# A hybrid SSD / DeltaNet layer on one core: the first two projection blocks read x itself, and u is formed in place while the second one runs

## The chip, the cores and the metric

The kernel runs on one core of a Trainium2 chip. The metric is the device time of one execution in microseconds (us). Five instruction streams run side by side and wait for each other through semaphores: TensorE (PE), VectorE (DVE), ScalarE (ACT), GpSimd (POOL) and SyncE (SP), which issues most of the DMAs.

## The reference, cut to what matters

Only the start of the layer is touched: the RMS norm of the input, and the first columns of the one input projection. 336 tokens (16 meta, 256 prompt, 64 sample) of 2048 channels go in.

```python
def _rmsnorm(x, w):
    xf = xf * lax.rsqrt(jnp.mean(xf * xf, axis=-1, keepdims=True) + EPS)
    return (xf * w.astype(jnp.float32)).astype(x.dtype)
...
    u = _rmsnorm(x, norm_mix_w)
    z_a, xbc_a, dt_a, qkv_b, z_b, beta_b, a_b, gate_a, gate_b = jnp.split(u @ w_in, SPLIT_IDX, axis=-1)
    xbc, conv_a_new = _causal_conv(xbc_a, conv_a, ssd_conv_w, ssd_conv_b)
    xbc = jax.nn.silu(xbc).astype(f32)
```

With r the root of a token and w the norm weight, u = x * r * w. So u @ W equals r times (x @ (w * W)): the weight can go into W, and the root, which is one number for each token, can be applied to the product.

## The kernel before

Everything that PE multiplies in the big projections is split in two: a float32 value v becomes hi (v rounded to fp32r by ACT) and lo (v - hi by DVE), and a product is three matmuls, hi*hi, hi*lo and lo*hi. The stream of weights is cut in chunks `n` of 512 rows by 256 columns. `wload(n)` issues the DMA of a chunk into a tile `raw` on SP, and `wsplit(n)` makes `hi` (one ACT instruction) and `lo` (one DVE instruction) of it. There are three buffers each of `raw`, `hi` and `lo`, so chunk n is loaded when the `lo` of chunk n-3 has been formed. `block()` multiplies four chunks (16 k of 128 channels) by the transposed activations `uh`, `ul` (channels on partitions, 336 tokens) into two PSUM tiles `pbig`: 24 matmuls for a chunk, 96 for a block. The first block of all takes the k in order with both column tiles in turn; later ones take the four k of a chunk for one column tile and then for the other.

`proj_ssd(0)`, the generator `main0`, runs five such blocks: two for the x part of the first SSD group (they end in a convolution, `conv_a`), one for B and C, two for z. The first block is interleaved by hand with the preparation (under `manual_schedule`, so all engines keep the written order there); from the second block on `run(main0, side)` puts steps of `side` between the matmuls, by the numbers that `side` yields, PE keeps the written order, and a scheduler decides the order on the other engines.

The preparation: x is loaded in three pieces of 112 tokens, transposed on PE (`flip`) and copied into `xT`; the sums of squares (`sumsq`) go through `root` (a power on POOL) and `spread_d` (a diagonal matrix `dgx` on DVE) to PE, which spreads the roots over all partitions (`prx`, copied to `rbx`). Then, for each k, `u_scale` multiplies `xT` by `rbx` (on DVE for even k, on POOL for odd k) and `u_split` forms `uh` (ACT) and `ul` (DVE). Only then can the matmuls of that k start. Behind the first block come the transposes of the convolution weights and states (`load_cols` of `cra`, `crb`, `sra`, `srb`), the 32 matmuls `ptok` for the small dt/beta/a columns, and then the second block. `tokens()` turns `ptok` into decays (`pcum`, `prow`), writes them to DRAM (`rowd`, DMA on ACT) and the scan of the first group reads them back (`eab`, `em`), with the SSD state `sio` behind them on SP (PE turns it: `psi`). `scratch()` writes `xT` to DRAM (`xTd`) for the residual.

## Time and profile before

| | us |
|---|---|
| median of 3 runs | 2344.87 (2339.98 to 2345.06) |
| the profiled execution | 2343.37 |
| its span | 2341.5 |
| PE busy in the span | 2300.9 (98%) |
| DVE / ACT / POOL busy | 1354.5 / 1065.4 / 333.1 |
| first matmul of the first block starts | 21.36 |
| last matmul of the first block starts | 46.54 |

PE is busy for nearly the whole span; it is not in the first 48 us. A profile row gives start, duration, engine, source line, operation, output and input tiles, and in brackets how long the engine sat idle before it and what ended that. A duration can hold time in which the instruction was stalled after its start.

### The profile page before, as it was taken

The page shows a single profiled execution, that of the slowest core. Times are in us where ns is not written, and L with a number is a line of the kernel's source. Part 1 is how long each engine was busy: PE and PEld are TensorE (multiplying, and loading weights), DVE is VectorE, ACT ScalarE, POOL GpSimd, SP SyncE. Part 2 cuts the span into 40 slices and gives each one's busy share as a digit, 9 for nine tenths or more (in the row PEclk, how much of TensorE's full clock was granted, in tenths as well). Part 3 has the DMA queues.
Part 4 walks back from the last instruction along what each step waited for, and adds up shares of the span by engine and source line. Part 5 has one row for each costly group of instructions (what it writes and reads, how often), then busy time and mean ns, then how long its engine had stood idle before and what let it go on. Part 6 is the DMA issues. An engine that isn't in the chain of part 4 may idle for free.

```text
span 2341.5 us, 40643 instructions
## 1 busy us (share of the span) xinstructions
PE 2300.9 (98%) x16393; PEld 2278.7 (97%) x16393; DVE 1354.5 (58%) x2147; ACT 1065.4 (46%) x1830; POOL 333.1 (14%) x488
## 2 busy tenths in 40 slices
PE   7999999999999999999999999999999999999997
PEld 6999999999999999999999999999999999999997
DVE  6675757575765547668668567444444444444444
ACT  5664545455445545554554445433343244234433
POOL 3142414141121112112212110000000000000000
PEclk9999999999999999999999999999999999999999
DMA  7845454546565555645556644544544454445543
GB/s 193 224 131 161 136 174 126 173 124 179 157 199 172 151 163 137 163 147 144 144 149 161 171 142 145 151 150 151 148 152 153 146 152 153 146 152 151 166 143 117
DMA packets 411046, 362.87 MB, mean 155 GB/s; under 512 B 48329, under 2 KB 407834, under 8 KB 410394
## 3 DMA queue, kind: packets, MB, share of 16 engines
q1 hardware_dynamic: 410746, 360.15, 52.8%
q8 instruction: 128, 2.10, 0.4%
...
q10 hardware_dynamic: 112, 0.13, 0.0%
...
## 4 chain that ended last, share of the span: by engine, by line
PE 90%; DVE 5%; DMA 2%; ACT 1%; issue 1%; SPq 1%; POOL 0%; ACTq 0%; DVEq 0%
PE pbig L58 84%; DVE lo L64 1%; DMA raw<-in_w_in_dram 1%; PE po L58 1%; DVE pr L64 1%; DVE ubt L858 1%; PE pS L58 0%; DVE c L67 0%; PE pyd L58 0%; PE pw L58 0%; PE pkk L58 0%; PE pqk L58 0%; ACT hi L61 0%; PE ph L58 0%; DMA x<-in_x_sample_dram 0%
## 5 line engine op out<-in xcount | busy, mean ns | idle before, releaser
L64 DVE TENSOR_TENSOR lo<-raw,hi 128x1024 fp32r<-128x1024 f32 x591 | 738.2, 1250 | 711.2 <-ACT hi L61 705.1
L61 ACT ACTIVATE hi<-raw 128x1024 fp32r<-128x1024 f32 x592 | 627.5, 1060 | 890.4 <-PE pbig L58 840.1
L58 PE MATMUL pbig<-uh,hi 128*128 128x320 f32 (+2 forms) x2176 | 689.2, 317 | 4.2 <-ACT uh L61 4.2
L58 PE MATMUL pbig<-ul,hi 128*128 128x320 f32 (+2 forms) x2176 | 682.5, 314 | 4.0 <-DVE ul L67 3.9
L58 PE MATMUL pbig<-uh,lo 128*128 128x320 f32 (+2 forms) x2176 | 681.0, 313 | 0.7 <-DVE lo L64 0.7
L58 PEld LDWEIGHTS pbig<-uh,hi 128*128 128x128 f32 x2176 | 411.3, 189 | 10.0 <-ACT uh L61 4.7
L58 PEld LDWEIGHTS pbig<-ul,hi 128*128 128x128 f32 x2176 | 411.5, 189 | 6.0 <-DVE ul L67 5.8
L58 PEld LDWEIGHTS pbig<-uh,lo 128*128 128x128 f32 x2176 | 411.4, 189 | 1.0 <-DVE lo L64 1.0
L58 PE MATMUL pbig<-hh,hi 128*128 128x320 f32 x1024 | 318.0, 311 | 0.0
L58 PE MATMUL pbig<-hnl,hi 128*128 128x320 f32 x1024 | 317.1, 310 | 0.0
L58 PE MATMUL pbig<-hl,hi 128*128 128x320 f32 x1024 | 316.2, 309 | 0.0
L58 PE MATMUL pbig<-hh,lo 128*128 128x320 f32 x1024 | 316.2, 309 | 0.0
L58 PE MATMUL pbig<-hnh,lo 128*128 128x320 f32 x1024 | 315.8, 308 | 0.0
L58 PE MATMUL pbig<-hnh,hi 128*128 128x320 f32 x1024 | 315.1, 308 | 0.0
L58 PEld LDWEIGHTS pbig<-hnh,lo 128*128 128x128 f32 x1024 | 192.9, 188 | 0.0
L58 PEld LDWEIGHTS pbig<-hl,hi 128*128 128x128 f32 x1024 | 192.6, 188 | 0.0
L58 PEld LDWEIGHTS pbig<-hh,hi 128*128 128x128 f32 x1024 | 192.6, 188 | 0.0
L58 PEld LDWEIGHTS pbig<-hnh,hi 128*128 128x128 f32 x1024 | 192.3, 188 | 0.2
L58 PEld LDWEIGHTS pbig<-hh,lo 128*128 128x128 f32 x1024 | 192.5, 188 | 0.0
L58 PEld LDWEIGHTS pbig<-hnl,hi 128*128 128x128 f32 x1024 | 192.2, 188 | 0.0
L58 PE MATMUL pbig<-yh,hi 128*128 128x320 f32 x512 | 161.2, 315 | 1.1 <-ACT yh L61 1.1
L58 PE MATMUL pbig<-yl,hi 128*128 128x320 f32 x512 | 157.6, 308 | 0.3 <-DVE yl L64 0.3
...
## 6 DMA issues: line engine op xcount, KB each, us to landing
raw<-in_w_in_dram SPq DMA_DIRECT2D x256, 512.0 KB, 3.9
raw<-in_w_up_dram SPq DMA_DIRECT2D x128, 512.0 KB, 3.9
raw<-in_w_down_dram SPq DMA_DIRECT2D x128, 512.0 KB, 3.5
...
raw<-in_w_in_dram SPq DMA_DIRECT2D x32, 256.0 KB, 3.5
...
```

The source lines that it names most:

```text
L58: nc.tensor.matmul(out, lhsT=lhsT, rhs=rhs, start=start, stop=stop, **kw)
L61: nc.scalar.activation(out=out, in_=in_, func=func, **kw)
L64: eng.tensor_tensor(out=out, in0=a, in1=b, op=op)
L858: V.tensor_reduce(out=ubt[:NE, j0:, s], in_=v, axis=AX.X, op=ADD)
```

## The change: what it does

- The first two blocks (chunks 0 to 7, `NRAW = 8`) multiply x, not u. `flip` now forms `uh` and `ul` straight from the transposes in PSUM (ACT, then DVE). `wsplit` of these eight chunks puts the norm weight into hi and lo: four ACT and four DVE instructions of 256 columns, one for each k, where there was one of 1024 each.
- The root is applied at the end of the two blocks: `conv` gets `rb=rbx` and multiplies the PSUM tiles by `rbx` on DVE, where ACT copied them.
- x comes in pieces of 128, 128 and 80 tokens, the last one in two halves of its columns. Chunk 0 is loaded ahead of the last piece. The small rows (`prow`, and the convolution weights and states) are loaded first, by DMAs on ACT, and are turned between the transposes of x. `warmer` puts 6, 3 and 3 matmuls of the identity on PE.
- `whole_x` makes `xT` (x itself) again as uh + ul on POOL, four instructions of 1344 columns. The sums of squares, `root` and `spread` now lie between the matmuls of the first block.
- `renorm`, a side generator ahead of `tokens()`, forms u in `uh` and `ul` while the second block runs: for each k a product by `rbx` (POOL, every fourth on DVE), `uh` on ACT, `ul` on DVE, each over the k that the second block has used up. `ptok` moves into `tokens()`, behind `renorm`.

```diff
         lo = wpool.tile([P, 4, 256], F32R, tag="lo", name="lo", bufs=3)
-        tt(G if n == 3 else V, lo, raws[n], hi.bitcast(F32), SUB)
+        if n < NRAW:
+            for k in range(4):
+                w = par[:, NM + n % 4 * 4 + k:NM + n % 4 * 4 + k + 1]
+                act(hi[:, k, :], raws[n][:, k, :], AF.Copy, scale=w)
+                stt(lo[:, k, :], raws[n][:, k, :], w, hi[:, k, :].bitcast(F32), MUL, SUB)
+        else:
+            act(hi, raws[n])
+            tt(V, lo, raws[n], hi.bitcast(F32), SUB)
         split[n] = hi, lo
+    NRAW = 2 * KD // 4
...
-    segs = [[(0, "meta", 0, 16), (16, "pr", 0, 96)], [(0, "pr", 96, 112)], [(0, "pr", 208, 48), (48, "sa", 0, 64)]]
+    X_LO, XS = (0, P, 2 * P), (P, P, NT - 2 * P)
+    segs = [[(0, "meta", 0, 16), (16, "pr", 0, 112)], [(0, "pr", 112, 128)], [(0, "pr", 240, 16), (16, "sa", 0, 64)]]
     src = {"meta": i["meta_tokens"], "pr": i["x_prompt"][0], "sa": i["x_sample"][0]}
-    def load_x(n):
+    xs = [xp.tile([P, D], F32, name=f"x{n}") for n in range(3)]
+    HD = D // 2
+    def load_x(n, c0=0, c1=D):
         for p0, s, r0, nr in segs[n]:
-            nc.sync.dma_start(xs[n][p0:p0 + nr, :], src[s][r0:r0 + nr, :])
-    for n in range(3):
-        xs.append(xp.tile([112, D], F32, name=f"x{n}"))
+            nc.sync.dma_start(xs[n][p0:p0 + nr, c0:c1], src[s][r0:r0 + nr, c0:c1])
...
+    prow = sp0.tile([73, P], F32, name="prow")
+    for r0, name, nr in ((NM, "norm_mix_w", 16), (SN, "ssd_norm_w", 16), (NP_, "norm_mlp_w", 16), (CB_, "ssd_conv_b", 24), (GN, "gdn_norm_w", 1)):
+        nc.scalar.dma_start(prow[r0:r0 + nr, :], i[name][0].rearrange("(t c) -> t c", c=P))
+    turned = []
+    for dst, source, n in ((cwa, i["ssd_conv_w"][0], 96), (sta, i["state_ssd_conv"][0, 0], 72), (cwb, i["gdn_conv_w"][0], 96), (stb, i["state_gdn_conv"][0, 0], 72)):
+        flat = source.rearrange("k (t c) -> (k t) c", c=P)
+        cols = dst.rearrange("p k t -> p (k t)")
+        for r0 in range(0, flat.shape[0], n):
+            row = sp0.tile([96, P], F32, name=f"row{len(turned)}")
+            nc.scalar.dma_start(row[:n, :], flat[r0:r0 + n, :])
+            turned.append((cols[:, r0:r0 + n], row, n))
     load_x(0)
     load_x(1)
-    prow = sp0.tile([73, P], F32, name="prow")
-    for r0, name, nr in ((NM, "norm_mix_w", 16), (SN, "ssd_norm_w", 16), (NP_, "norm_mlp_w", 16), (CB_, "ssd_conv_b", 24), (GN, "gdn_norm_w", 1)):
-        nc.sync.dma_start(prow[r0:r0 + nr, :], i[name][0].rearrange("(t c) -> t c", c=P))
-    load_x(2)
-    warm = sp0.tile([P, 1], F32, name="warm")
-    act(warm, ones[:, 0:1], AF.Square)
+    wload(0)
+    load_x(2, 0, HD)
+    load_x(2, HD, D)
+    wload(1)
+    wload(2)
...
+    def warmer(n):
+        ps = scr("pwarm")
+        for _ in range(n):
+            mm(ps[:, :P], ident, ident)
...
+    def flip(n, k):
+        x0, w = X_LO[n], XS[n]
+        ps = scr("pu").rearrange("p (k t) -> p k t", k=4)[:, :, :w]
+        for m in range(4):
+            transp(ps[:, m, :], xs[n][:w, (k + m) * P:(k + m + 1) * P])
+        h, l = uh[:, k:k + 4, x0:x0 + w], ul[:, k:k + 4, x0:x0 + w]
+        act(h, ps)
+        tt(V, l, ps, h.bitcast(F32), SUB)
...
+        r = rsx[:XS[n], n:n + 1]
+        V.tensor_scalar(out=r, in0=ssx[:XS[n], n:n + 1], scalar1=1.0 / D, scalar2=EPS, op0=MUL, op1=ADD)
+        tt(G, r, r, nhalf_pow[:XS[n], 0:1], ALU.pow)
+        V.tensor_scalar(out=dgx[:XS[n], n, :XS[n]], in0=ident[:XS[n], :XS[n]], scalar1=r, scalar2=None, op0=MUL)
+    def spread():
+        prx = scr("prx")
+        for n in range(3):
+            mm(prx[:, X_LO[n]:X_LO[n] + XS[n]], ones[:XS[n], :], dgx[:XS[n], n, :XS[n]])
+        act(rbx, prx[:, :NT])
+    un = [flat[:, k * NT:(k + 1) * NT] for k in range(KD - 1)] + [sp0.tile([P, NT], F32, name="un")]
...
+    def whole_x(q):
+        tt(G, xT[q], uh[:, q * 4:q * 4 + 4, :].bitcast(F32), ul[:, q * 4:q * 4 + 4, :].bitcast(F32), ADD)
+    def renorm():
+        yield 4.9
+        for k in range(KD):
+            w = par[:, NM + k:NM + k + 1]
+            tt(V if k % 4 == 3 else G, un[k], xT[k // 4][:, k % 4, :], rbx, MUL)
+            act(uh[:, k, :], un[k], AF.Copy, scale=w)
+            stt(ul[:, k, :], un[k], w, uh[:, k, :].bitcast(F32), MUL, SUB)
+            yield 1.0
...
+        if rb is None:
+            act(t[:, 3 + n0:275], ps[:, 0:272 - n0])
+            act(t[:, 278:342], ps[:, 272 - n0:336 - n0])
+        else:
+            tt(V, t[:, 3:275], ps[:, 0:272], rb[:, 0:272], MUL)
+            tt(V, t[:, 278:342], ps[:, 272:336], rb[:, 272:336], MUL)
...
-                conv_a(pt[j], g * 4 + b * 2 + j, x4[:, b * 2 + j, :])
+                conv_a(pt[j], g * 4 + b * 2 + j, x4[:, b * 2 + j, :], 0, None if g else rbx)
...
-    for k in range(4):
-        u_scale(k)
+    warmer(6)
+    load_cols(par, prow, 73)
+    for t in turned[:2]:
+        load_cols(*t)
+    for k in range(0, KD, 4):
+        flip(0, k)
+    for t in turned[2:]:
+        load_cols(*t)
+    warmer(3)
+    for k in range(0, KD, 4):
+        flip(1, k)
+    wsplit(0)
+    warmer(3)
+    flip(2, 0)
+    flip(2, 4)
     for k in range(KD):
-        u_split(k)
-        if k + 4 < KD:
-            u_scale(k + 4)
-        if k % 4 == 1 and k < KD - 4:
-            wsplit(k // 4 + 1)
         for _ in range(2 if k < KD - 1 else 1):
             next(main0)
+        if k == 0:
+            wsplit(1)
+        elif k == 1:
+            flip(2, 8)
+        elif k == 2:
+            flip(2, 12)
+            sumsq(act, 0)
+        elif k == 3:
+            sumsq(V, 1)
+            for q in range(4):
+                whole_x(q)
+            root(0)
+        elif k == 4:
+            wsplit(2)
+            sumsq(act, 2)
+        elif k == 7:
+            root(1)
+            wsplit(3)
+        elif k == 9:
+            root(2)
+        elif k == 12:
+            spread()
+            wsplit(4)
     manual.close()
     hold[0] = len(stream)
...
+        yield 8.0
+        ptok = scr("ptok")
+        for n in range(2):
+            w, wr = wt[:, n * 8:(n + 1) * 8, :], sp.tile([P, 8, P], F32R, tag="wtr", name="wtr", bufs=2)
+            act(wr[:, :, 0:64], w)
+            tt(V, wr[:, :, 64:], w, wr[:, :, 0:64].bitcast(F32), SUB)
+            for k in range(8):
+                mm(ptok[:, :NT], wr[:, k, :], uh[:, n * 8 + k, :], n == 0 and k == 0, False)
+                mm(ptok[:, :NT], wr[:, k, :], ul[:, n * 8 + k, :], False, n == 1 and k == 7)
+        tokT = sp.tile([P, NT], F32, name="tokT")
+        act(tokT, ptok[:, :NT])
+        yield 2.0
...
-    run(main0, chain(tokens(), scratch()))
+    run(main0, chain(renorm(), tokens(), scratch()))
```

**Where the roots are formed.** DVE in the changed kernel, in the first block, from the last split of x to the `lo` of chunk 2 (`lo_381`); `dgx` is the diagonal of the first piece's roots:

```order
L64 TENSOR_TENSOR ul_88<-pu_350,uh_87 128x4x80 [waits Activation_49]
L364 SCALAR_TENSOR_TENSOR acc_89,ssx_187<-x1_146 128x2048 [waits DMAHW4_49]
L368 TENSOR_SCALAR rsx_188<-ssx_187 128x1 [waits Activation_49]
L370 TENSOR_SCALAR dgx_189<-ident_74,rsx_188 128x128 [waits Pool_49]
L67 SCALAR_TENSOR_TENSOR lo_381<-raw_181,par_90,hi_380 128x256 [waits DMAHW4_49,Activation_49]
```

POOL at the same place; the two last kinds of row are the powers of the roots for which `dgx` waits:

```order
L64 TENSOR_TENSOR xT_183<-uh_87,ul_88 128x1344 [waits DVE_49]
L64 TENSOR_TENSOR xT_184<-uh_87,ul_88 128x1344 [waits DVE_49]
L64 TENSOR_TENSOR xT_185<-uh_87,ul_88 128x1344 [waits DVE_49]
L64 TENSOR_TENSOR xT3_186<-uh_87,ul_88 128x1344 [waits DVE_49]
L64 TENSOR_TENSOR rsx_188<-rsx_188,nhalf_pow_83 128x1 [waits DVE_49] x2
L64 TENSOR_TENSOR rsx_188<-rsx_188,nhalf_pow_83 80x1 [waits DVE_49]
```

Before, the roots stood ahead of the first block on both engines, with no 1344-column instruction on POOL and no `lo` of a running block behind a `dgx`. Now `lo_381` stands behind the first `dgx`, which stands behind a power that stands behind all four `whole_x`.

**The start of the second block.** DVE in the changed kernel, from the first row that uses `rbx`: `acc` is the scaled x of k = 3 and 7, `lo_465` is chunk 4, `pre` takes the finished first block, `lo_536` is chunk 5, `c` is the convolution:

```order
L64 TENSOR_TENSOR acc_89<-xT_183,rbx_190 128x336 [waits Activation_49]
L67 SCALAR_TENSOR_TENSOR lo_465<-raw_372,par_90,hi_464 128x256 [waits DMAHW1_49,PE_49,Activation_49]
L64 TENSOR_TENSOR acc_89<-xT_184,rbx_190 128x336
L67 SCALAR_TENSOR_TENSOR lo_465<-raw_372,par_90,hi_464 128x256 [waits Activation_49] x3
L64 TENSOR_TENSOR pre0_116<-pbig_311,rbx_190 128x272 [waits PE_49]
L64 TENSOR_TENSOR pre0_116<-pbig_311,rbx_190 128x64
L64 TENSOR_TENSOR pre1_117<-pbig_312,rbx_190 128x272 [waits PE_49]
L64 TENSOR_TENSOR pre1_117<-pbig_312,rbx_190 128x64
```

And directly behind these:

```order
L67 SCALAR_TENSOR_TENSOR lo_536<-raw_422,par_90,hi_535 128x256 [waits DMAHW3_49,Activation_49]
L67 SCALAR_TENSOR_TENSOR c_512<-pre0_116,cwa_91,c_512 128x339 [waits Activation_49]
L67 SCALAR_TENSOR_TENSOR lo_536<-raw_422,par_90,hi_535 128x256
L67 SCALAR_TENSOR_TENSOR c_512<-pre0_116,cwa_91,c_512 128x339 [waits DVE_49]
L67 SCALAR_TENSOR_TENSOR c_524<-pre1_117,cwa_91,c_524 128x339 [waits Activation_49]
L67 SCALAR_TENSOR_TENSOR c_512<-pre0_116,cwa_91,c_512 128x339 [waits DVE_49]
L67 SCALAR_TENSOR_TENSOR c_524<-pre1_117,cwa_91,c_524 128x339 [waits DVE_49]
L67 SCALAR_TENSOR_TENSOR lo_536<-raw_422,par_90,hi_535 128x256
L67 SCALAR_TENSOR_TENSOR c_524<-pre1_117,cwa_91,c_524 128x339 [waits DVE_49]
L67 SCALAR_TENSOR_TENSOR lo_536<-raw_422,par_90,hi_535 128x256
```

Before, these `lo` were one instruction each and the convolution of the first block came between whole ones. Now the quarters of chunk 5 lie between single steps of the convolution, with five of these ahead of the third quarter; POOL runs its twelve products by `rbx` in the same stretch.

**The loads of x.** SP before, from its start:

```order
L293 DMA x0_145<-in_meta_tokens_dram 16x2048
L293 DMA x0_145<-in_x_prompt_dram 96x2048
L293 DMA x1_146<-in_x_prompt_dram 112x2048
L301 DMA prow_151<-in_norm_mix_w_dram 16x128
L301 DMA prow_151<-in_ssd_norm_w_dram 16x128
```

SP in the changed kernel, from its start:

```order
L304 DMA x0_145<-in_meta_tokens_dram 16x2048
L304 DMA x0_145<-in_x_prompt_dram 112x2048
L304 DMA x1_146<-in_x_prompt_dram 128x2048 [waits DMAHW4_49]
L198 DMA raw_173<-in_w_in_dram 128x4x256 [waits DMAHW6_49]
L304 DMA x2_147<-in_x_prompt_dram 16x1024 [waits DMAHW7_49]
L304 DMA x2_147<-in_x_sample_dram 64x1024 [waits DMAHW0_49]
```

The second piece of x now waits for a DMA semaphore, `DMAHW4`, on which PE also waits ahead of the transposes of the first piece; everything else on SP stands behind it.

## Rows read from the trace of the kernel before

**Rows 1.** The page, part 1: busy us, share, instructions.
```profile
PE 2300.9 (98%) x16393; PEld 2278.7 (97%) x16393; DVE 1354.5 (58%) x2147; ACT 1065.4 (46%) x1830; POOL 333.1 (14%) x488
```

**Rows 2.** Windows of the span: busy us (instructions) by engine, PEclk, DMA share, GB/s.
```profile
20.00:30.00 10.00, 7.85 (x37) 7.07 (x38) 9.86 (x13) 7.81 (x15) 6.81 (x6) 0.83 0.30 80
40.00:50.00 10.00, 7.43 (x37) 6.98 (x38) 5.07 (x15) 5.10 (x11) 0.95 (x4) 0.83 1.12 273
...
110.00:120.00 10.00, 10.00 (x73) 9.98 (x71) 3.28 (x3) 5.63 (x7) 0.00 (x0) 1.00 0.59 169
```

**Rows 3.** Waits of PE, 0 to 150 us: total us, times, longest.
```profile
PE pbig L58 <- ACT uh L61: 4.2, 2, 2.3
PE pbig L58 <- DVE ul L67: 3.9, 4, 2.1
...
PE pcum L58 <- DVE la L64: 0.5, 1, 0.5
```

**Rows 4.** Timeline of PE: the first block, its spacing, its end, and what follows.
```profile
21.36 0.42 PE L58 MATMUL pbig<-uh,hi 128*128 128x336 f32 x1 [2.30 <-ACT uh L61]
...
28.05 0.32 PE L58 MATMUL pbig<-uh,lo 128*128 128x336 f32 x1
28.20 0.32 PE L58 MATMUL pbig<-ul,hi 128*128 128x336 f32 x1
...
46.54 0.32 PE L58 MATMUL pbig<-ul,hi 128*128 128x336 f32 x1
...
48.40 0.40 PE L58 MATMUL ptok<-uh,wtr 128*128 128x336 f32 x1
```

**Rows 5.** Timeline of PE: the first transposes of two pieces of x.
```profile
6.91 1.73 PE L87 MATMUL pu<-ident,x 112*128 112x112 f32 x16 [1.64 <-DMA x<-in_x_prompt_dram]
10.12 1.72 PE L87 MATMUL pu<-ident,x 112*128 112x112 f32 x16 [1.48 <-DMA x<-in_x_prompt_dram]
```

**Rows 6.** Timeline of SP: the issue of the prompt's rows of both pieces.
```profile
1.26 0.87 SPq L293 DMA_DIRECT2D x<-in_x_prompt_dram  x2
```

**Rows 7.** Timeline of DVE and ACT: durations of instructions that the change uses.
```profile
7.53 1.16 DVE L351 COPY xT<-pu 128x448 f32<-128x448 f32 x2 [7.53 <-PE pu L87]
...
10.00 2.29 DVE L326 SCALAR_TENSOR_TENSOR acc<-x 112x2048 f32<-112x2048 f32 x1 [0.94 <-DMA x<-in_x_prompt_dram]
...
10.72 1.85 ACT L61 ACTIVATE xT<-pu 128x448 f32<-128x448 f32 x4 [0.85 <-PE pu L87]
...
17.32 0.28 DVE L340 TENSOR_SCALAR dgx<-ident,rsx 112x112 f32<-112x112 f32 x1 [0.29 <-POOL rsx L64]
...
17.54 1.22 DVE L64 TENSOR_TENSOR lo<-raw,hi 128x1024 fp32r<-128x1024 f32 x1
...
31.79 1.04 DVE L67 SCALAR_TENSOR_TENSOR ul<-ut,par,uh 128x336 fp32r<-128x336 f32 x2
```

**Rows 8.** Timeline of DVE, from 32.7 us.
```profile
32.75 1.23 DVE L64 TENSOR_TENSOR ut<-xT,rbx 128x336 f32<-128x336 f32 x1
33.91 3.13 DVE L67 SCALAR_TENSOR_TENSOR ul<-ut,par,uh 128x336 fp32r<-128x336 f32 x2
```

**Rows 9.** Timeline of POOL: a power, three products, and a whole `lo`.
```profile
16.73 0.55 POOL L64 TENSOR_TENSOR rsx<-rsx,nhalf_pow 112x1 f32<-112x1 f32 x1 [3.61 <-DVE rsx L336]
19.62 3.47 POOL L64 TENSOR_TENSOR ut<-xT,rbx 128x336 f32<-128x336 f32 x3 [2.33 <-ACT rbx L61]
...
32.43 1.19 POOL L64 TENSOR_TENSOR ut<-xT,rbx 128x336 f32<-128x336 f32 x1 [1.34 <-DVE ul L67]
33.58 2.61 POOL L64 TENSOR_TENSOR lo<-raw,hi 128x1024 fp32r<-128x1024 f32 x1
```

**Rows 10.** Timeline: the decay rows' write on ACT, their first read on SP.
```profile
80.67 0.35 ACTq L586 DMA_DIRECT2D rowd<-rows  x1
...
83.46 0.58 SPq L612 DMA_DIRECT2D eab<-rowd  x1
```

**Rows 11.** DMA issues by line: count, KB, us to landing.
```profile
sio<-in_state_ssd_dram SPq DMA_DIRECT2D x4, 256.0 KB, 6.0
```

More of the change, by code (lines that the diff above doesn't have):

```diff
@@ L318, in tile_hybrid_step @@
+    ssx = sp0.tile([P, 3], F32, name="ssx")
+    rsx = sp0.tile([P, 3], F32, name="rsx")
+    dgx = sp0.tile([P, 3, P], F32, name="dgx")
     rbx = sp0.tile([P, NT], F32, name="rbx")
-    HD = D // 2
-    def sumsq(f, x, d0, n):
-        d = junk[:, d0:d0 + x.shape[1]]
+    def flip(n, k):
[6 more added lines that the diff above has]
+        tt(V, l, ps, h.bitcast(F32), SUB)
@@ L323, in sumsq @@
+    def sumsq(f, n):
+        x, d, s = xs[n][:XS[n], :], flat[:XS[n], n % 2 * D:(n % 2 + 1) * D], ssx[:XS[n], n:n + 1]
         if f is act:
-            act(d, x, AF.Square, accum_out=ssx[:, n:n + 1])
+            act(d, x, AF.Square, accum_out=s)
         else:
-            V.scalar_tensor_tensor(out=d, in0=x, scalar=1.0, in1=x, op0=MUL, op1=MUL, accum_out=ssx[:, n:n + 1])
-    def flip(n, k):
-        ps = scr("pu").rearrange("p (k t) -> p k t", k=4)[:, :, :112]
-        for m in range(4):
-            transp(ps[:, m, :], xs[n][:, (k + m) * P:(k + m + 1) * P])
-        return xT[k // 4][:, :, n * 112:(n + 1) * 112], ps
@@ L334, in root @@
-    def root(n):
-        r = rsx[:, n:n + 1]
-        V.tensor_scalar(out=r, in0=ssx[:, n:n + 1], scalar1=1.0 / D, scalar2=EPS, op0=MUL, op1=ADD)
-        tt(G, r, r, nhalf_pow[:112, 0:1], ALU.pow)
-    def spread_d(n):
-        V.tensor_scalar(out=dgx[:, n, :], in0=ident[:112, :112], scalar1=rsx[:, n:n + 1], scalar2=None, op0=MUL)
-    manual = ExitStack()
-    manual.enter_context(tc.manual_schedule())
-    pw_ = scr("pwarm")
-    for n in range(8):
-        mm(pw_[:, :P], ident, ident)
-    prx = psb.tile([P, 512], F32, tag="big", name="prx")
@@ L349, in tile_hybrid_step @@
-    sumsq(act, xs[0], 0, 0)
-    for k in range(0, KD, 4):
-        (V.tensor_copy if k < 8 else act)(*flip(0, k))
-    root(0)
-    sumsq(V, xs[1], D, 1)
-    for k in range(0, KD, 4):
-        act(*flip(1, k))
-    root(1)
-    load_cols(par, prow, 73)
-    for n in range(3):
-        wload(n)
-    sumsq(act, xs[2][:, :HD], 0, 2)
-    sumsq(V, xs[2][:, HD:], D, 3)
-    tt(V, ssx[:, 2:3], ssx[:, 2:3], ssx[:, 3:4], ADD)
-    root(2)
-    spread_d(0)
-    spread_d(1)
-    act(*flip(2, 0))
-    late = [flip(2, k) for k in (4, 8, 12)]
@@ L368, in tile_hybrid_step @@
-    spread_d(2)
-    wsplit(0)
-    for n in range(3):
-        mm(prx[:, n * 112:(n + 1) * 112], ones[:112, :], dgx[:, n, :])
-    act(rbx, prx[:, :NT])
-    for a in late:
-        act(*a)
-    xctx.close()
-    sp = start.enter_context(tc.tile_pool(name="sp", bufs=1))
-    ut = {}
-    def u_scale(k):
-        ut[k] = sp0.tile([P, NT], F32, tag="ut", name="ut", bufs=6)
-        tt(G if k % 2 else V, ut[k], xT[k // 4][:, k % 4, :], rbx, MUL)
-    def u_split(k):
-        t, w = ut.pop(k), par[:, NM + k:NM + k + 1]
-        act(uh[:, k, :], t, AF.Copy, scale=w)
-        stt(ul[:, k, :], t, w, uh[:, k, :].bitcast(F32), MUL, SUB)
+            V.scalar_tensor_tensor(out=d, in0=x, scalar=1.0, in1=x, op0=MUL, op1=MUL, accum_out=s)
@@ L504, in tile_hybrid_step @@
     nc.sync.dma_start(wt[:, :, 32:64], win[:, C_BETA:C_BETA + 32].rearrange("(k p) c -> p k c", p=P))
-    ptok = psb.tile([P, 512], F32, tag="big", name="ptok")
-    for n in range(2):
-        w, wr = wt[:, n * 8:(n + 1) * 8, :], wpool.tile([P, 8, P], F32R, tag="hi", name="wtr", bufs=3)
-        act(wr[:, :, 0:64], w)
-        tt(V, wr[:, :, 64:], w, wr[:, :, 0:64].bitcast(F32), SUB)
-        for k in range(8):
-            mm(ptok[:, :NT], wr[:, k, :], uh[:, n * 8 + k, :], n == 0 and k == 0, False)
-            mm(ptok[:, :NT], wr[:, k, :], ul[:, n * 8 + k, :], False, n == 1 and k == 7)
-    tokT = sp.tile([P, NT], F32, name="tokT")
-    act(tokT, ptok[:, :NT])
-    def tokens():
-        yield 1.0
+    def tokens():
+        yield 8.0
[10 more added lines that the diff above has]
+        yield 2.0
         for c in range(3):
```

38 lines of the change are left out of this document (10 added, 28 removed).

## The prediction

> **What bounds the kernel now.** I read the busy table first: PE is busy for 98% of the span [rows 1], so over most of the 2341.5 us only less work on PE could help, and the change takes none away. What it can win is PE's idle time at the start. There, the timeline of PE shows the first block's first matmul at 21.36 us and its last one at 46.54 [rows 4]. The block is 96 matmuls that follow each other every 0.155 us at full clock [rows 4], so 14.9 us of work lasted 25.5. The list of PE's waits says for what: for `uh` on ACT (4.2 us, of which 2.3 stand ahead of the first matmul) and for `ul` on DVE (3.9) [rows 3]. The windows show the rest: in 20 to 30 and in 40 to 50 us the granted clock is 0.83, so part of each stretch ran at the lower level (1.2 GHz, not 2.4), which costs 0.17 x 10 = 1.7 us each time [rows 2], both times behind a pause of PE. Behind the block the conv transposes end only when `ptok` starts at 48.40 [rows 4]. From there on PE has work without a gap, but for 0.5 us ahead of `pcum` [rows 3]; a window at 110 us shows it full [rows 2].
>
> So I compare one point: the end of the second block, without `ptok` (which moves). Before it stands at 48.40 + 14.9, and with the later 0.5 us at **63.8 us**. Whatever the changed kernel reaches there earlier or later, it keeps to the end.
>
> **The start of the first block.** Before, x had to be whole and normed. Now the block waits for transposes and splits alone. The second piece of x decides. Before, both pieces were issued at 1.26 us [rows 6], and PE could turn them at 6.9 and 10.1 [rows 5]. Now the second piece's DMA waits for the first one's landing (the order on SP), at about 6.8 us, and then needs what the first needed, 6.91 - 1.26 = 5.65, for 1024 KB where that had 896: between 5.65 (the same) and 6.5 us (by size) more, I take 5.8. It lands at 12.6, 2.5 us later than before. Then DVE is the chain: four splits from PSUM of 512 columns at 0.66 each (a copy of 448 took 0.58; ACT's half of one is 0.46 [rows 7], and hidden), with 1.0 for PE and ACT ahead of the first; four quarters of `lo` at 0.40 (a 1024-column `lo` took 1.22 and a 336-column step 0.52, so 256 columns come to 0.45 in the row, 0.40 from start to start); two splits of 80 tokens at 0.45. 12.6 + 1.0 + 2.6 + 1.6 + 0.9 = 18.7 us. PE's first matmul comes at about 17.3, its third, which needs the last split, at 18.3. The first two chunks (2 x 3.7), two more transposes (0.6) and a low-clock stretch (1.7) take it to **27.7 us**. Up to here the change wins some 4 us.
>
> **Chunk 2 waits for the roots.** Its `lo_381` stands on DVE behind `dgx`, that behind a power on POOL, and that behind four `whole_x`. POOL and DVE take turns where both read two tiles in SBUF: at 32.75 a product on DVE of half a microsecond lasted 1.23 because POOL's was running, POOL's whole `lo` then seems to last 2.61, of which it waited 0.4 for that product, and DVE's next two steps last 3.13 in place of 1.04 [rows 8, 9, 7]. So POOL's 1024 columns cost 2.2, and three products of 336 that took turns with DVE's lasted 3.47 [rows 9], which leaves 0.7 for one once DVE's turns of 0.45 are taken off. From 336 to 1024 that is 2.1 ns a column: a `whole_x` of 1344 is an estimated 2.8 us. From 18.7 us on, one after the other because each blocks or waits for the next: `whole_x` 2.8, a quarter of chunk 1's `lo` 0.4, `whole_x` 2.8, three quarters 1.2, the split of x that the third `whole_x` needs 0.45, `whole_x` 2.8, DVE's sum of squares 2.3 [rows 7], `whole_x` 2.8, the power 0.55 [rows 9], `dgx` 0.3 [rows 7], the first quarter 0.4. Sum 16.8: `lo_381` is there at **35.5**, and PE has waited 7.8 us.
>
> Perfetto Trace Analysis, section GPSIMD Engine Instruction, of the Trainium skill says that a GpSimd span in a profile isn't to be trusted and that start-to-start spacing is. Taking the spans as they stand (2.61 for 1024 columns, so 3.4 for a `whole_x`) the four would cost 2.6 us more; [rows 8, 9] speak for the shorter price.
>
> Then come chunks 2 and 3 (7.4) and `prx` (0.65): block one ends at 43.5. `rbx` is ready 2.2 us earlier, at 41.3, because three k are still to be multiplied. The other two roots come in time: chunk 3's `lo` is formed by 39.
>
> **The second block.** From 41.3 on POOL runs its twelve products (0.7 each), and in DVE's order every step with two SBUF inputs takes a turn with them. DVE needs six such turns (the products for k = 3 and 7, the quarters of `lo_465`), some 6.1 to 6.8 us in all, before the fourth quarter is there; PE wants it after 3.9: 2.5 us of waiting. Then four products from PSUM (1.25, no turn), and the third quarter of `lo_536` stands behind two quarters and five steps of the convolution, with POOL's last five products in between: 14.6 us after `rbx`, the fourth at 15.6. PE, late as it already is, wants the fourth at 10.1: 5.3 us of waiting. From chunk 6 on DVE is ahead again. So the block takes 14.9 + 2.5 + 5.3 = 22.7, and ends at 66.2. The 8 extra quarter splits, the root on `pre` and the removed ACT copies cost nothing else: DVE has until the third block for them. In the third block `ul` of k = 11 is late by some 0.9 us.
>
> **Low clock.** PE now pauses for 7.8 us and later for 4.0 in one piece. Before, each low stretch cost 1.7 us and stood behind a pause of about 2 us, though not every such pause had one. I count one whole and one at half: 2.6, which takes up the 0.9 of the third block. Bounds 0.9 and 3.4.
>
> **The scan.** `ptok` and `tokens()` now come one and a half blocks later. `prow` then stands only 51 matmuls (7.5 us, at 0.148) ahead of `psi`. For `psi` the rows must be copied and written, then read: before, the first read was issued 2.8 us after the write [rows 10]; with 1.5 for the copies, two reads are issued at 4.3 after `prow`, and `sio` behind them at 5.5. `sio` lands between 2.8 (the time from the write to that read, the nearest short DMA) and 6.0 us later [rows 10, 11], at 8.3 to 11.5, and PE wants it at 8.0. I take 1.0 us, with bounds of 0 and 3.5.
>
> **Sum.** 66.2 + 2.6 + 1.0 - 63.8 = **+6.0 us** on the profiled execution's 2343.4 us: **2349.4 us**. That execution lies 1.5 us under the median of the runs shown, so I take its own time. A change under 0.3% (7 us) can't be told from none in a measurement of this kernel; the forecast is a slight loss inside that.
>
> **Rivals.**
> *Faster: POOL and DVE don't block each other.* Then `whole_x` 1 and 2 run beside the quarters, the third starts at 24.4, the last ends at 30.0, and with the power, `dgx` and a quarter `lo_381` comes at 31.2: PE waits 3.5, and in the second block 0.4. The point is reached at 31.2 + 8.05 + 15.3 = 54.6, with the clock's 1.7 to 56.3: -7.5, with the scan's 1.0 -6.5 to -8, some **2336 us**. It would take that the long rows on DVE had another cause. Against it: both directions are in [rows 8, 9], and the sums close. SBUF, section Who interferes with whom, of the Trainium skill states the lock as exclusive for a DVE instruction with two SBUF inputs against a GpSimd one that reads; the trace agrees, 3.13 for 1.04. For it: the overlap of the two engines is seen in few rows, none with an instruction as long as `whole_x`. Chance 0.17.
>
> *Slower: the state is late for `psi`.* Place: `prow`, `rowd`, `eab`, `sio`. If the reads take the 6.0 us that the page gives for `sio` [rows 11], PE waits 3.5 instead of 1.0, and a pause of that length can bring another low stretch (1.7): +4.2, **2353.6 us**. It decides from a landing later than 8.0 us after `prow`. Before, `prow` was two blocks and a half ahead, and nothing waited. Chance 0.23.
>
> *The change doesn't do what it says*, that is, PE's first matmul is no earlier: if the second piece lands 3 us later than I take, the chain shifts as a whole, +3: 2352. Chance 0.1; the loss is then the forecast's with another first term.
>
> *Forecast*, 0.5.
>
> **How the numbers follow.** The forecast has a spread of about 5 us (landing 1.5, clock 1.7, POOL's price 2, turns 2): some four tenths of its 0.5 lie above +7 us, which is 0.21, and six tenths of the second and third rivals' 0.33, which is 0.19: slower by over 0.3%, 0.40. Faster by over 0.3%: the first rival's 0.17 and 0.01 of the rest, 0.18. Within 0.3%: 0.42. The range, 2335 to 2357, reaches to the first rival's time and to the second's with its spread; 0.1 is left out at either end.
>
> **What would show it.** The second piece's transposes at 12 to 13.5 us; the first matmul at 16.5 to 18.5; a single wait of PE of 6 to 9 us in the middle of the first block, put down to DVE `lo`, with POOL's four 1344-column rows in front of it; a second group of waits for `lo`, 6 to 9 us in all, in the second block; `psi` waiting for a DMA. The forecast is wrong if POOL's rows lie beside DVE's full-speed rows (first rival), if the wait for `lo_381` is under 4 us, or if the first matmul comes before 15 us: each would bring the time under 2343. If the stalls are there and the time is still lower, I have missed an idle stretch of the kernel before.

## The result, and the profile after

The changed kernel takes **2362.93 us** (median of 4 runs, 2359.57 to 2366.08) against 2342.43 us of the kernel before on the same chip (2339.41 to 2345.06): ratio 1.0088, 95% interval 1.0063 to 1.0113. It is 20.5 us slower. The forecast, 2349.4 us, has the sign right and a third of the size; the result lies above its range.

The profiled execution took 2359.57 us with a span of 2357.8, that is 16.3 over the span of before. It is the fastest of its four runs, and the one of before was 0.9 above its median, so the traces account for 16.3 of the 20.5 us; the other 4 us are the spread between executions and have no row.

PE's waits in the first 160 us (the view of [rows 3]; total us, times, longest):

```profile
PE pbig L58 <- DVE lo L67: 14.8, 7, 7.5
PE psi L87 <- DMA em<-rowd: 4.6, 1, 4.6
PE pcol L87 <- DMA row<-in_gdn_conv_w_dram: 4.1, 2, 3.4
PE pcol L87 <- DMA row<-in_state_gdn_conv_dram: 1.9, 1, 1.9
```

Where they stand, in the timeline of PE ([rows 4, 5] are its counterpart; start, duration, and in brackets the idle time ahead and what ended it):

```profile
15.35 0.35 PE L87 MATMUL pcol<-ident,row 72*128 72x72 f32 x1 [1.92 <-DMA row<-in_state_gdn_conv_dram]
...
16.87 2.66 PE L87 MATMUL pu<-ident,x 128*128 128x128 f32 x16
...
22.23 0.42 PE L58 MATMUL pbig<-uh,hi 128*128 128x336 f32 x1 [1.39 <-ACT uh L61]
...
29.91 0.42 PE L58 MATMUL pbig<-uh,lo 128*128 128x336 f32 x1 [1.29 <-DVE lo L67]
...
40.49 0.65 PE L58 MATMUL pbig<-uh,lo 128*128 128x336 f32 x1 [7.53 <-DVE lo L67]
...
63.07 0.65 PE L58 MATMUL pbig<-uh,lo 128*128 128x336 f32 x1 [3.52 <-DVE lo L67]
...
74.47 0.31 PE L58 MATMUL pbig<-uh,hi 128*128 128x336 f32 x1
...
133.88 0.63 PE L87 MATMUL psi<-ident,sio 128*128 128x128 f32 x4 [4.57 <-DMA em<-rowd]
```

The second piece of x is turned at 16.87, behind the transpose of a row of convolution state that nothing in this sublayer's first blocks needs. The first matmul comes at 22.23, later than the 21.36 of before [rows 4]. The 7.53 us ahead of chunk 2 are the forecast's. The second block's last wait ends at 63.07. Its 96 matmuls are through when the third block's first one starts, at 74.47, and DVE starts on its convolution at 74.48.

That is the point which the prediction put at 63.8 for the kernel before. There it left out three matmuls of the first block, 0.5 us, which come only behind `ptok` (PE's timeline of before: the three from 53.42, then the second block):

```profile
53.42 0.32 PE L58 MATMUL pbig<-uh,hi 128*128 128x336 f32 x1
...
53.89 0.32 PE L58 MATMUL pbig<-uh,hi 128*128 128x336 f32 x1
```

With them the point of before is 64.3, and the changed kernel reaches it **10.2 us** later.

POOL and then DVE in the timeline ahead of 40.49 (what [rows 7, 9] gave the prices for):

```profile
23.27 6.30 POOL L64 TENSOR_TENSOR xT<-uh,ul 128x1344 f32<-128x1344 f32 x2 [14.17 <-DVE ul L64]
31.13 8.09 POOL L64 TENSOR_TENSOR xT<-uh,ul 128x1344 f32<-128x1344 f32 x2 [1.55 <-DVE ul L64]
39.18 0.55 POOL L64 TENSOR_TENSOR rsx<-rsx,nhalf_pow 128x1 f32<-128x1 f32 x1
```
```profile
23.50 7.14 DVE L67 SCALAR_TENSOR_TENSOR lo<-raw,par,hi 128x256 fp32r<-128x256 f32 x4
...
31.37 4.98 DVE L364 SCALAR_TENSOR_TENSOR acc<-x 128x2048 f32<-128x2048 f32 x1
...
39.76 0.28 DVE L370 TENSOR_SCALAR dgx<-ident,rsx 128x128 f32<-128x128 f32 x1 [3.34 <-POOL rsx L64]
```

Four quarters of `lo` last 7.14 us beside the first two `whole_x` (1.66 where POOL is idle), and the sum of squares 4.98 (2.3 alone, [rows 7]). The first power comes only at 39.18, behind all four.

The windows (the view of [rows 2]) show what the pause costs beyond itself. After the busy times of PE, PEld, DVE, ACT and POOL stand the granted clock, the DMA share and GB/s:

```profile
35.00:40.00 5.00, 0.00 (x0) 0.00 (x0) 1.66 (x5) 0.00 (x0) 4.72 (x2) 0.55 0.67 234
40.00:45.00 5.00, 4.50 (x16) 4.51 (x17) 3.67 (x13) 0.00 (x0) 1.10 (x2) 0.50 0.92 300
...
120.00:140.00 20.00, 15.43 (x98) 15.03 (x97) 8.30 (x18) 7.59 (x11) 1.67 (x3) 0.91 0.76 186
```

From 40 to 45 us PE works at half the clock (1.2 GHz); in the window with `psi` the clock is 0.91, or 1.8 us. From the second block's end to `psi` PE is full. `psi` starts 14.9 us later than before (133.88 against 118.96), which is the 10.2 and the wait of 4.6 to within 0.1.

The sum: 10.2 to the compared point, 4.6 and 1.8 at `psi`, and 2.4 of new waits in the first scan (1.3 ahead of `ph` from 167 to 169 us, 1.2 of `prb` for `dg` at 191.6; both are steps of the scan) make 19.0. A low clock behind the new waits (1.8 us between 190 and 210) is matched by one of before (1.8 between 380 and 420). The last `ph` of these scans agrees: it starts at 532.4 against 512.9, 19.5 later. The kernel before then lost 2.4 us to a clock of 0.96 between 1140 and 1200 us that this execution did not; with that, 17.1 stand beside the 16.3 measured.

### The profile page after: what moved, and what is told of

It reads as the page before. It is cut to its first block, busy times and chain, and to the rows that moved or that the text cites. A ratio compares the mean times of both kernels' runs of the same rounds, so it can differ in the third digit from the quotient of the medians.

```text
span 2357.8 us, 40730 instructions
## 1 busy us (share of the span) xinstructions
PE 2303.2 (98%) x16401; PEld 2280.3 (97%) x16401; DVE 1371.7 (58%) x2183; ACT 1069.0 (45%) x1848; POOL 347.6 (15%) x495
## 4 chain that ended last, share of the span: by engine, by line
PE 91%; DVE 4%; DMA 2%; ACT 1%; issue 1%; POOL 1%; SPq 0%; ACTq 0%; DVEq 0%
PE pbig L58 84%; DVE c L67 1%; PE po L58 1%; DVE lo L67 1%; DVE lo L64 1%; DMA em<-rowd 1%; PE pS L58 0%; PE pw L58 0%; PE pkk L58 0%; PE pqk L58 0%; PE pyd L58 0%; POOL xT L64 0%; PE ph L58 0%; PE pks L58 0%; PE pu L58 0%
## 5 line engine op out<-in xcount | busy, mean ns | idle before, releaser
L64 DVE TENSOR_TENSOR lo<-raw,hi 128x1024 fp32r<-128x1024 f32 x584 | 729.3, 1250 | 704.6 <-ACT hi L61 697.1
L61 ACT ACTIVATE hi<-raw 128x1024 fp32r<-128x1024 f32 x584 | 618.1, 1058 | 886.2 <-PE pbig L58 841.2
L58 PEld LDWEIGHTS pbig<-uh,lo 128*128 128x128 f32 x2176 | 411.6, 189 | 17.9 <-DVE lo L67 16.8
```

What stands on the lines that cost most here:

```text
L58: nc.tensor.matmul(out, lhsT=lhsT, rhs=rhs, start=start, stop=stop, **kw)
L61: nc.scalar.activation(out=out, in_=in_, func=func, **kw)
L64: eng.tensor_tensor(out=out, in0=a, in1=b, op=op)
```

## The experiments

Each is measured against the kernel before, run on the same chip in the same session. a to d, f to i, j to m and n to p ran on four different chips, so across these groups the ratios are to be compared rather than the times. The changed kernel itself is the first row; times are medians.

| run | us | ratio to before | interval | span of the profile |
|---|---|---|---|---|
| changed | 2362.93 | 1.0088 | 1.0063 to 1.0113 | 2357.8 |
| a_roots_first | 2363.08 | 1.0091 | 1.0078 to 1.0105 | 2359.0 |
| b_rows_late | 2355.12 | 1.0062 | 1.0048 to 1.0076 | 2353.6 |
| c_products_dve | 2360.00 | 1.0076 | 1.0063 to 1.0090 | 2356.6 |
| d_psi_late | 2361.28 | 1.0081 | 1.0069 to 1.0093 | 2359.6 |
| f_sums_dve | 2360.01 | 1.0083 | 1.0070 to 1.0096 | 2357.4 |
| g_prow_early | 2355.11 | 1.0061 | 1.0049 to 1.0073 | 2354.2 |
| h_f_b_g | 2361.15 | 1.0084 | 1.0070 to 1.0097 | 2359.0 |
| i_f_b_c_g | 2359.21 | 1.0076 | 1.0064 to 1.0088 | 2360.2 |
| j_dvec_row | 2360.78 | 1.0091 | 1.0074 to 1.0109 | 2358.9 |
| k_f_b_g_dvec | 2346.24 | 1.0025 | 1.0015 to 1.0034 | 2344.9 |
| l_f_b_c_g_dvec | 2347.26 | 1.0027 | 1.0018 to 1.0036 | 2341.7 |
| m_b_g_dvec | 2349.69 | 1.0046 | 1.0030 to 1.0062 | 2346.0 |
| n_k_spread | 2347.57 | 1.0027 | 1.0015 to 1.0038 | 2348.0 |
| o_l_spread | 2349.47 | 1.0044 | 1.0031 to 1.0056 | 2350.5 |
| p_before_dvec | 2336.15 | 0.9985 | 0.9976 to 0.9994 | 2332.2 |

### The late rows (b)

```diff
-    for t in turned[2:]:
-        load_cols(*t)
     warmer(3)
...
+        elif k == 13:
+            for t in turned[2:]:
+                load_cols(*t)
```

> The two transposes of convolution rows that only the second sublayer needs move from ahead of the second x piece's transposes to k = 13 of the first block. Theory one: in the changed kernel the second piece's transposes came at 16.9 us, 3.3 later than its landing at about 13.6, because PE stood at a row's transpose that waited for its DMA. Then they come at 13.5 to 14.2 us, the first matmul at 19 to 20 instead of 22.2, and since the roots' chain starts at a split of x, everything up to block one's end comes 2.5 to 3 us earlier: 2359 to 2361 us. Theory two: the piece itself lands late; then the transposes come no earlier than 16 us, and the time stays within 1 us of 2362.9.

PE's timeline:

```profile
12.95 2.10 PE L87 MATMUL pu<-ident,x 128*128 128x128 f32 x16
...
17.79 0.42 PE L58 MATMUL pbig<-uh,hi 128*128 128x336 f32 x1 [0.69 <-ACT uh L61]
...
36.18 0.65 PE L58 MATMUL pbig<-uh,lo 128*128 128x336 f32 x1 [7.55 <-DVE lo L67]
```

It is theory one, and by more than it said. The piece had landed by 12.95; the first matmul moves from 22.23 to 17.79, and the wait ahead of chunk 2 keeps its 7.5 us and moves with it, from 40.49 to 36.18. The loss falls from 0.88% to 0.62%, some 6 us by the medians and 4.2 by the spans.

### The order on POOL (a)

```diff
             sumsq(V, 1)
-            for q in range(4):
-                whole_x(q)
             root(0)
...
             root(2)
+            for q in range(4):
+                whole_x(q)
```

> The four sums of uh and ul on POOL (whole_x) move from k = 3 to k = 9 of the first block, behind the third root's power; nothing else changes. Theory one: PE's 7.5 us of waiting for lo ahead of chunk 2 and most of the 10 us at the low clock around it come from the order on POOL's queue, where the first power stands behind four whole_x. Then the wait falls under 2 us, block one ends near 43 us instead of 51.8, and since the renorm products keep their distance from the block's end, the second block still waits 5 to 8 us: the end of the second block comes at 64 to 67 us instead of 74.3, the time to 2350 to 2355 us. Theory two: the turns that DVE takes with whole_x cost the wait, wherever whole_x stands. Then at least 4 us of the waiting is found again in chunks 2 and 3, and the time stays at 2358 us or more.

Neither theory named what happened. Chunk 2 no longer waits, so the order on POOL did cause that wait. But the time is unchanged, because PE now stands 11.2 us ahead of `prx`. POOL, DVE and PE there:

```profile
35.68 11.93 POOL L64 TENSOR_TENSOR xT<-uh,ul 128x1344 f32<-128x1344 f32 x4
```
```profile
35.74 11.92 DVE L370 TENSOR_SCALAR dgx<-ident,rsx 80x80 f32<-80x80 f32 x1 [0.66 <-POOL rsx L64]
```
```profile
47.71 0.72 PE L58 MATMUL prx<-dgx,ones 80*128 80x80 f32 x2 [11.23 <-DVE dgx L370]
```

The third `dgx`, 0.26 us of work, starts 0.06 us behind the first `whole_x` and ends with the fourth. So POOL holds DVE at both places of the sums. What that costs can't be read from a alone: f below shows that without the hold weight chunks would have been late in the same stretch.

### POOL's products (c)

```diff
-            tt(V if k % 4 == 3 else G, un[k], xT[k // 4][:, k % 4, :], rbx, MUL)
+            tt(V, un[k], xT[k // 4][:, k % 4, :], rbx, MUL)
```

> The twelve products un = x * rbx that POOL makes in the second block go to DVE, which makes all sixteen. Theory one: POOL and DVE exclude each other where both read two tiles in SBUF, so that a product on POOL costs DVE about its whole length (0.7 us) while one on DVE costs 0.45. Then DVE gets ahead by up to 12 x 0.25 = 3 us, and PE's 6.0 us of waiting in the second block falls to 3 to 5: 2360 to 2362 us. Theory two: the two engines work mostly side by side, and the second block's waits are DVE's load alone; then DVE has 12 x 0.45 = 5.4 us more to do, the waits grow to 9 to 11.5 us, and the time goes to 2366 to 2369 us.

PE's waits from 45 to 95 us, where the changed kernel has 6.0 us, all for `lo`:

```profile
PE pbig L58 <- ACT uh L61: 3.4, 1, 3.4
PE pbig L58 <- DVE ul L67: 0.9, 1, 0.9
PE pbig L58 <- DVE lo L67: 0.2, 1, 0.2
```

It is theory one: with more to do and no POOL beside it DVE is earlier, and the second block waits 0.2 us. But u is formed later, and the third block waits 4.3 for it. Most of the gain is handed on.

### `psi` later, or `prow` earlier (d, g)

d:

```diff
-        yield 14.0 if g else 4.0
+        yield 14.0
```

> In the first scan the transposes of the state (psi) come 14 instead of 4 us of PE's work behind the issue of its reads, as in the other three scans. Theory one: the changed kernel brought prow so close to psi that PE waits 4.6 us for the reads and loses 1.5 to 2 us more at the low clock behind that pause; with other matmuls in between both vanish, nothing takes their place, and the time falls by 5 to 6.5 us to 2356.5 to 2358 us. Theory two: the scan behind psi is itself a chain that PE has too little other work to cover; then the wait comes back at pcb, pxt or at the scan's end, and the time stays at 2361 us or more.

g:

```diff
-        yield 15.5
+        yield 11.0
         pcum = scr("pcum")
```

> The cumulative sums of the scan's decays, and prow with them, come 11.0 instead of 15.5 us of PE's work behind the token rows, so 4.5 us earlier, with psi where it is. Theory one: psi waits because prow is only 7.5 us of matmuls ahead of it, so the reads of rowd land late, and moving psi instead only pushed the scan's own chain past the end of the work beside it (a 5.0 us wait at prs). Then psi's wait falls from 4.6 us to under 1, the low clock behind it goes, no wait comes at prs, and the time falls by 5 to 7 us to 2356 to 2358 us. Theory two: psi waits for a load that does not hang on prow (the state itself behind other transfers). Then its wait stays over 3 us, and the time within 2 us of 2362.9.

In the changed kernel the chain is, on ACT's queue and on SP's ([rows 10] before):

```profile
122.66 0.35 ACTq L610 DMA_DIRECT2D rowd<-rows  x1
```
```profile
124.89 1.25 SPq L636 DMA_DIRECT2D eab<-rowd  x2
126.19 0.60 SPq L646 DMA_DIRECT2D sio<-in_state_ssd_dram  x1
126.84 1.06 SPq L641 DMA_DIRECT2D em<-rowd  x2
```

d removes the wait at `psi`, and a wait of 5.0 us comes up at `prs`, between 160 and 260 us, "`prs` for POOL `sq`", at the scan's end. That is theory two: the scan's chain has too little other work beside it. g removes the wait at `psi` without a new one (PE is busy for 20.00 of the 20 us from 120 to 140, at full clock), and takes the loss from 0.88% to 0.61%. So `psi` hung on `prow`, and the mend is an earlier `prow`. By its row `psi` reads only `sio`; whether it waits for `em`, as the view has it, or for `sio`, which is issued between the two reads of `rowd`, no run separates.

### The sums on DVE (f, h, i)

```diff
-        tt(G, xT[q], uh[...], ul[...], ADD)
+        tt(V, xT[q], uh[...], ul[...], ADD)
...
-            for q in range(4):
-                whole_x(q)
             root(0)
...
             root(2)
+            wsplit(4)
+            for q in range(4):
+                whole_x(q)
         elif k == 12:
             spread()
-            wsplit(4)
```

> The four sums of uh and ul (whole_x) are made by DVE instead of POOL, and stand in DVE's order behind the third root and the weight split of chunk 4 (which moves from k = 12 to k = 9). Theory one: what cost PE its 7.5 us of waiting, the low clock behind it and, with the sums merely moved back on POOL, the 11.2 us ahead of prx, is that POOL holds what DVE needs while it sums. Then block one runs with waits under 2 us in all from its first matmul at 22.2 us, ends at 39 to 41 us instead of 51.8, the second block still waits 5 to 8 us behind POOL's products, and ends at 62 to 65 instead of 74.3: 2349 to 2353 us. Theory two: the first block is bound by DVE's own work, and 5.8 us more of it (four sums of some 1.45 us) put the wait at chunk 2, at prx or at the second block's start: waits of 8 us or more up to there, 2358 us or more.

f had waits of 13.6 us up to the second block's end: no gain, as theory two has it, but not for its reason alone. On ACT the split of chunk 4 waits for the chunk itself:

```profile
40.63 1.71 ACT L61 ACTIVATE hi<-raw,par 128x256 fp32r<-128x256 f32 x4 [6.15 <-DMA raw<-in_w_in_dram]
```

DVE stands idle for 4.75 us behind that, and its four sums come later still. So the late weights, which h shows at their worst, cost here already. h adds b's and g's edits to f; i adds c's as well.

> Three changes in one: the sums on DVE behind the roots, the late rows' transposes at k = 13, the cumulative sums at 11.0. If the three costs are separate, their gains add: 10 to 12 us for the first, 4 to 4.5 for the second, 5 to 6 for the third, from 2362.9 us to 2340 to 2344 us, about the kernel before. If they hide one another (one chain behind all three), the sum falls short by more than 4 us: 2347 us or more.

> As the combination of three, and all sixteen products of the renorm on DVE besides, so that POOL and DVE never read pairs of tiles beside each other in the first two blocks. If the turns still cost PE 5 us or more in the second block of the combination, this gains 2 to 4 us on it, to 2337 to 2341 us, with waits for uh in the third block of up to 5 us. If DVE's load decides by then (sixteen products and sixteen formations of ul at some 0.5 us are 15.5 us, the block's own length), the waits grow and it loses 2 us or more.

h, ACT's and PE's timelines, and the two loads of `dvec` in the list of DMA issues (last figure: us to landing):

```profile
44.18 1.71 ACT L61 ACTIVATE hi<-raw,par 128x256 fp32r<-128x256 f32 x4 [14.70 <-DMA raw<-in_w_in_dram]
...
49.86 0.43 ACT L61 ACTIVATE rbx<-prx 128x336 f32<-128x336 f32 x1
```
```profile
50.34 0.38 PE L87 MATMUL pcol<-ident,row 72*128 72x72 f32 x1 [17.06 <-ACT rbx L61]
```
```profile
dvec<-in_ssd_d_dram SPq DMA_DIRECT2D x2, 4.0 KB, 22.4
```

ACT waits 14.7 us for a weight chunk that is issued behind `dvec`, and `rbx` stands behind that chunk's split and a quarter of the next one on ACT. The two loads of 4 KB take 22.4 us to land, and from 25 to 35 us the DMA engines move nothing. In the changed kernel this lay hidden under PE's wait for the sums (j below). i differs from h mainly in the second block (1.6 us of waiting for `lo` in place of 7.3), as in c.

### The loads in 4-byte elements (j, k, l, m, p)

```diff
-    for h in range(2):
-        nc.sync.dma_start(dvec[h * 64:(h + 1) * 64, :], i["ssd_d"][0].rearrange("(t h) -> h t", h=2)[h].partition_broadcast(64))
+    nc.sync.dma_start(drow, i["ssd_d"][0].partition_broadcast(P))
+    for h in range(2):
+        V.tensor_copy(dvec[h * 64:(h + 1) * 64, :], drow[h * 64:(h + 1) * 64, :].rearrange("p (t h) -> p h t", h=2)[:, h, :])
```

j is the changed kernel with this alone, k is h with it, l is i with it, m has it with b's and g's edits and the sums still on POOL, p is the kernel before with this alone.

> The two loads that spread ssd_d over 128 partitions in 4-byte elements (dvec, 64 x 16 each) become one load of 128 rows of 128 bytes and two small copies on DVE; the rest is the changed kernel. In it the queue on SP moves nothing between 20 and 25 and between 30 and 36 us with the dvec loads in it, and a raw chunk of weights issued behind them lands only at 40 us or later. Theory one: those loads hold the queue, but the changed kernel doesn't feel it, since PE waits for POOL and DVE over the same stretch: the idle stretches of the queue go, and the time stays within 2.5 us of 2362.9. Theory two: the late weights are part of PE's waits already: 2357 us or less.

> The combination of three (sums on DVE behind the roots, late rows at k = 13, cumulative sums at 11.0) with the one-row load of ssd_d. With the sums off POOL, PE waited 17.1 us for rbx instead, whose ACT step stood behind a weight split that waited 14.7 us for its raw chunk. Theory one: the 4-byte loads hold that chunk back. Then hi waits under 2 us, prx's result is there at 34 to 36 us, the second block ends at 57 to 62 us (63.8 in the kernel before), and the time is 2337 to 2344 us. Theory two: the chunk is late for the writes of zeros and the ring behind the x pieces, whatever dvec does. Then at least 8 us of that wait stays, and the time at 2352 us or more.

> As k, with all sixteen products of the renorm on DVE. If POOL's products still cost turns in the second block, its waits (5 to 9 us in k) fall to 1 to 4, and the time is 2 to 4 us under k's; if DVE's load decides, it is 1 us or more over k's.

> The changed kernel with the late rows at k = 13, the cumulative sums at 11.0 and the one-row load of ssd_d, but the sums left on POOL at k = 3. If the first two gains add (each took 7 to 8 us off the median, 4 off the span of its profile) the time is 2347 to 2351 us, with the wait for lo ahead of chunk 2 at 7.5 us as before and 5 to 7 us of waits in the second block; the difference to k is then what the sums on POOL cost: 6 to 10 us.

> The kernel before with the one-row load of ssd_d alone. In its trace the queue on SP moves nothing from 29 to 36 us with a dvec load in it, but no wait of PE is put down to a load of weights behind it. If nothing hangs on it the time is within 1.5 us of the kernel before; if the late weights do cost there, 2 us or more less.

j: no change, theory one: in the changed kernel the late weights are covered. k: 2346.2 us, 15 less than h, with no wait of PE for `hi` or `rbx`. So the loads were next in line behind the sums. The gain falls 2 us short of what theory one gave, for DVE now has the sums ahead of the next `lo`. k, DVE and PE:

```profile
34.02 5.96 DVE L64 TENSOR_TENSOR xT<-uh,ul 128x1344 f32<-128x1344 f32 x4
...
46.60 4.60 DVE L67 SCALAR_TENSOR_TENSOR c<-pre,cwa,c 128x339 f32<-128x339 f32 x4
```
```profile
43.67 0.42 PE L58 MATMUL pbig<-uh,lo 128*128 128x336 f32 x1 [3.30 <-DVE lo L67]
46.73 0.65 PE L58 MATMUL pbig<-uh,lo 128*128 128x336 f32 x1 [2.33 <-DVE lo L67]
52.28 0.65 PE L58 MATMUL pbig<-uh,lo 128*128 128x336 f32 x1 [4.34 <-DVE lo L67]
```

m, 2349.7, is as expected, and its distance to k is 3.5 us, not 6 to 10: the sums on POOL cost that much over the same sums on DVE, since they are work wherever they stand. The intervals of the two just overlap, so 3.5 is a rough figure. l has less waiting than k and the same time within its interval.

p is the version that beats both kernels: 0.9985 (0.9976 to 0.9994), 3.5 us under the kernel before by the ratio and 4.5 by the medians; `ptok` starts at 44.46 us in it, where it started at 48.40 [rows 4]. Against p the best form of the change, k, is still 0.4% slower. The window from 30 to 35 us, before and in p (last figure GB/s):

```profile
30.00:35.00 5.00, 3.48 (x21) 2.92 (x20) 5.00 (x7) 1.79 (x3) 3.66 (x3) 1.00 0.05 0
```
```profile
30.00:35.00 5.00, 3.94 (x24) 3.45 (x23) 5.00 (x8) 2.91 (x7) 3.42 (x3) 1.00 0.94 189
```

The loads held the queue before the change as well, and cost there too, but not through weights. On ACT of the kernel before, a small step for the decays (`nega`) stands ahead of the last four `uh`, and waits for one of the small loads behind `dvec`:

```profile
40.76 0.24 ACT L61 ACTIVATE nega<-pb 128x48 f32<-128x48 f32 x1 [7.81 <-DMA pb<-in_gdn_a_log_dram]
```

PE's second wait for `uh` [rows 3], 1.9 us ahead of 41.52, stands behind it, and behind that the low clock from 40 to 50 us [rows 2]. In p `nega` starts at 33.81 without a wait; PE doesn't wait there, and the clock is 1.00 from 40 to 50. So the list of PE's waits names the engine that came last, and the cause stood one step further back.

The edit also moved the load in SP's order. In j and k the one row is issued behind weight chunks (at 40.44 and 29.46), where the first `dvec` stood at 15.23 in the changed kernel, so these two don't separate the small elements from the place in the queue. In p it is issued at 22.04, between the places of the two `dvec` before (11.55 and 26.56); a run with the old loads at the new place was not made.

### The order of DVE's work (n, o)

n is k, o is l with

```diff
             wsplit(4)
-            for q in range(4):
+            for q in range(2):
                 whole_x(q)
...
             spread()
+            wsplit(5)
+            whole_x(2)
         elif k == 13:
+            whole_x(3)
```

> As k, but two of the four sums on DVE stand behind the weight split of chunk 5, which moves up to k = 12 of the first block. In k the wait for lo in the second block is 10.0 us in three pieces (3.3, 2.3, 4.3) at 43 to 52 us. Theory one: the first 5.6 us of it are the sums, ahead of chunk 5's lo on DVE. Then they go, the last 4.3 us, which stand behind convolution steps that take turns with POOL's products, stay or grow to 7, and the time falls by 2 to 4 us, to 2342 to 2344. Theory two: DVE has more to do up to the end of the second block than PE, in whatever order. Then the waits keep their sum within 2 us, and the time stays within 1.5 us of 2346.2.

> As n, with all sixteen products of the renorm on DVE. If POOL's products make the convolution's steps on DVE slow (1.15 us each in k, 0.49 where POOL is idle), the waits in the second block fall to 1 to 4 us, some come up for uh in the third, and the time is 2338 to 2342 us, at or under the kernel before. If DVE's load decides, it is no better than n.

n: the waits ahead of chunk 5 go (1.2 and 0.3 left) and the last one grows to 7.3; the time is k's. o's one wait for `lo` is 4.3, and its convolution steps run at full speed:

```profile
45.45 3.06 DVE L67 SCALAR_TENSOR_TENSOR c<-pre,cwa,c 128x339 f32<-128x339 f32 x6 [1.60 <-ACT c L61]
```

That is 0.51 each, against 1.15 in k. Yet o is no faster. Its windows tell why it differs from l, whose 60 to 80 us are at full clock (l first, then o):

```profile
60.00:80.00 20.00, 16.50 (x102) 15.05 (x101) 19.28 (x36) 12.73 (x26) 4.74 (x9) 1.00 0.58 180
```
```profile
60.00:80.00 20.00, 15.61 (x75) 13.66 (x74) 17.32 (x35) 10.56 (x19) 2.04 (x6) 0.83 0.44 137
```

Both miss some 4 us of PE there, now for u in the third block, and o loses 2.7 us of its busy time to the clock on top. So k, l, n and o trade the place of a loss that stays. Theory two of n reads it so that DVE has more to do up to the third block than PE; the runs agree with that, and don't prove it. That u could be formed in place without it in some other arrangement isn't excluded; none of the four did.

## Why the prediction was wrong in size

**The first matmul (17.3 forecast, 22.23 measured): the step that failed most.** "With 1.0 for PE and ACT ahead of the first" took PE to be free when the second piece landed. The landing was right (12.6 forecast; in o PE waits for the piece until 12.23). But in the changed kernel PE's written order has rows of the convolution ahead of it, and the last of these lands only at 15.35. Their DMAs, which the change moves to ACT's queue, stand nowhere in the sum. With the rows moved (b) the first matmul came at 17.79. This is about 5 us, and it carries through, since the chain of the roots hangs on the last split.

**Chunk 2's wait (7.8 forecast, 7.53 measured): right**, and its chain too: 16.8 us from the last split, at 23.6, to the first quarter of `lo`, at 40.4. The first rival, that POOL and DVE don't block each other, is excluded by the 11.92 us of a's `dgx` and by c.

**The second block (22.7 forecast, 23.6 measured, from 50.87 to 74.47): near in sum**; the waits were 6.0 for 7.8, and the low clock behind the last of them and slower matmuls right after each made up for more than that.

**Low clock: too small.** 2.6 us up to the end of the second block was about what the stretch at 40 to 45 cost (0.50 of 4.5 us, and a little ahead and behind), but each later pause brought its own: some 1.2 us between 60 and 70 (in the 23.6 above), 1.8 at `psi`.

**The scan (1.0 forecast, bounds 0 to 3.5; 4.57 measured): right place, low end taken.** PE wanted `psi` 8.1 us after `prow`, as forecast (8.0). `sio` was out at 126.19, 5.0 us after `prow` (5.5 forecast), and the read of `em` behind it, which has no term in the sum, at 126.84. PE got on 7.7 us after the one and 7.0 after the other, where the row at hand gave 6.0 for a landing [rows 11] and the nearest short DMA 2.8. The one row that was a landing should have carried the sum.

**The compared point:** 63.8 was 0.5 too early, as shown above, so this made the forecast's loss 0.5 too large.

**Not counted:** 2.4 us of waits between 167 and 192, and the 4 us between profile and median.

**The slower rival** ("the state is late for `psi`") happened, beside the forecast and not in its place; so did the third rival's shift of the whole chain. The forecast's own loss and these two add, for which the chances, one for each alone, left no room.
